# A hybrid RWKV and attention layer: strict order in the RWKV preparation, late output weights split on VectorE, a joint to the up phase without GpSimd

## The chip, the cores and the metric

The kernel runs on one core of one Trainium2 chip. A core has five engines that run side by side: TensorE (PE in the profile, with weight loads apart as PEld), VectorE (DVE), ScalarE (ACT), GpSimd (POOL) and SyncE (SP), which here only issues DMA transfers. The metric is device time in microseconds (us) of one execution. The kernel before took a median of 1824.77 us over three runs (1822.93 to 1825.58).

## The reference

One layer of a decoder trunk, for 1024 tokens of width 1024, in fp32:

```python
h = rms_norm(x, norm1_g)
proj = h @ w_in                       # RWKV, stick-breaking, memory query, gates
y_a = rwkv7_branch(p_rwkv, ...)       # token shift, decay, delta-rule state, 8 heads x 64
y_b = stick_breaking_branch(p_sb, ...)           # 8 heads x 64
y_m = memory_branch(q_mem, mem, ...)             # 256 memory tokens, 4 heads x 128
branch_out = einsum('btnc,ncd->btnd', stack(y_a, y_b, y_m), w_branch)
gates = sigmoid(gate_logits)
x = x + sum(gates * branch_out, axis=2) @ w_out
x = x + conv_ffn(x, ...)   # norm, w_up (5632), causal conv of width 3, silu(gate) * value, w_down
```

In the RWKV branch each token has a decay, a receptance r, a key k, a value v and a normalised key direction kk; the state is updated by `S = S*w + (S @ -kk) (kk*a) + v k`, and the output also gets a bonus, `sum(r*k*r_k) * v`, before a gate g.

## The kernel before

**Arithmetic.** Every large product is made of three products in the fast fp32r type: an operand is split into a high part, rounded by ACT (`Copy` into an fp32r tile), and a low part, the difference, made by DVE or POOL. `mm3` issues high x high, high x low and low x high. A 128 x 1024 weight tile is loaded by SP (`load_w`), rounded by ACT and differenced by POOL (`split_raw`, L82).

**Stages.** After a start of some 50 us, `rwkv_prep` runs four cycles, one for each pair of heads (p = 0 to 3), each a Python generator. `weave` runs it one step at a time, and after each step it takes one step of a filler stream, the projections of `x`: a filler step is mostly six matmuls, one eighth of a projection's contraction, and eight of them end a projection. So PE has six filler matmuls for each `yield` in `rwkv_prep`. From 310 us on attention, memory attention, gates and the RWKV state run in the same manner (the middle), then `branch_last` and `out_proj`, then the joint, where the up projection of the ConvFFN begins while the last tokens are still being normalised, and from about 1235 us a steady up phase and the down phase.

**One preparation cycle.** `k`, `a`, the decay and its running sum `cc` (a scan on DVE) give P and Q (exponentials on ACT). A column sum on PE, a power on POOL and `expand_heads` on DVE give the key's norm; `bcast_heads` broadcasts it over rows by eight transposes on PE (L113) into PSUM. Then DVE makes `kk` (L386) and `b` (L387). For each half h of the 1024 tokens `chain` makes two operands, `bk` (four multiplies of 64 x 512, L396) and `ra` (L397 to L399), and `gram` multiplies them, eight small matmuls for each quarter f, into PSUM, which DVE multiplies by a mask (L413) and three DMAs write out. `decayed` (POOL, L425) and `turned` (eight transposes) make a transposed operand. The bonus is two matmuls, two multiplies (L446) and a fused add (L447). `shifted` (L257) drains a projection: two multiplies out of PSUM (L263), an ACT scale, and the token shift's last operation on DVE (L266), here called the tail. All PSUM tiles that are not projections share one tag `g` of four banks.

**What sets the order.** A scheduler places the instructions of each engine by dependence and priority. `pinned` (L115) keeps a marked instruction in the program's order, and while `strict` is set it also chains it behind the last pinned one of its engine; before, `strict` was set only for the state stage. Most of PE's work is pinned. [...]

**Output weights.** `load_wo(k)` loads and splits the eight `w_out` tiles; the last four (k from 4) are loaded late and their lows run on POOL. `branch_last` ends with the merge: DVE multiplies the branch product by the gate (L1230), adds (L1235) and makes lows (L1242, tile `mg`).

**Up phase.** `w_up` is multiplied by a two-level Strassen-like scheme: for a pair n of weight tiles seven products, written (n,1) to (n,7), each 12 matmuls of 128 x 512. Their activations are the operands `11`, `21`, `22`, `T1` to `T4`, made by sums of quarters (L1310) and split by `high` (ACT) and `low` (L1325, DVE or POOL); their names in the profile are `B` or `BT`. Weight sums (`sums2`, `sums3`) and splits (`hl`, L1415) run on POOL. `step(n, i)` issues a product and what drains it; `conv` makes the convolution and the activation. The joint is the hand-written sequence at the end of `up_phase` that runs pairs 0 and 1.

## Time and profile before

| | |
|---|---|
| median of 3 runs | 1824.77 us |
| the profiled execution | 1822.09 us |
| its span | 1820.3 us |
| mean granted PE clock | 0.996 of full speed |
| instructions | 27424 |

A row of a timeline gives the start, the duration, engine, line, operation, output and inputs with their shapes, how often, and in brackets the idle time before it with what ended it. Equal neighbouring instructions are drawn together as one row (x2, x24), whose duration is the whole stretch. A matmul row's duration is modelled and overlaps the next, so the cost of one is read from the distance between starts. A row of the view of waits gives the waiting engine and line, what it waited for, the sum in us, how often, and the longest.

### The profile page before, as it was taken

The numbers are of one execution on the slowest core, as the hardware profiler recorded it, in microseconds if no ns is written. First come the engines' busy times: TensorE is split into PE (matmuls) and PEld (weight loads), VectorE is DVE, ScalarE is ACT, GpSimd is POOL, SyncE is SP. The second block draws the span as 40 slices with busy tenths as digits, with TensorE's granted clock in tenths as the row PEclk, the third lists the DMA queues.
The fourth block names the chain that finished last, engine by engine and source line by source line (L and its number), as shares of the span: only waits on it lengthen the run. The fifth ranks groups of instructions, "written<-read, shape, count | busy, mean of one in ns | idle before, by whom it ended". The sixth has DMA issues, their size and how long they took to land.

```text
span 1820.3 us, 27424 instructions
## 1 busy us (share of the span) xinstructions
PE 1784.4 (98%) x10468; PEld 1444.0 (79%) x10468; DVE 1191.1 (65%) x1659; ACT 882.7 (48%) x1665; POOL 770.1 (42%) x441
## 2 busy tenths in 40 slices
PE   8999999999999999999999999989999999999999
PEld 6777778878888888787777878868888888888887
DVE  5657773988977515232634792597776777786497
ACT  5443352555666645543556543464444444544343
POOL 2322343222221362221333341476777767645454
PEclk9999999999999999999999999999999999999999
DMA  4155466111112352457864562323332333386475
GB/s 182 59 174 185 146 191 221 50 42 50 58 41 79 103 162 65 154 190 243 283 230 182 204 213 105 127 61 113 110 110 87 101 114 110 122 298 240 145 236 203
DMA packets 120613, 263.39 MB, mean 145 GB/s; under 512 B 28313, under 2 KB 40857, under 8 KB 120354
## 3 DMA queue, kind: packets, MB, share of 16 engines
q1 hardware_dynamic: 82722, 194.76, 32.6%
q10 hardware_dynamic: 33984, 54.27, 8.1%
q0 software_dynamic: 3776, 12.62, 2.2%
q8 instruction: 82, 1.34, 0.3%
q14 instruction: 49, 0.40, 0.1%
HBM read 180.04 MB, written 81.53 MB: 144 GB/s over the span
## 4 chain that ended last, share of the span: by engine, by line
PE 77%; DVE 12%; issue 4%; ACT 3%; POOL 2%; DMA 2%; ACTq 0%; SPq 0%; DVEq 0%; POOLq 0%
PE mm L130 63%; PE g L130 11%; PE g L113 3%; POOL dw L1687 1%; DVE it L479 1%; DVE at L872 1%; DVE inst L481 1%; DVE qk L396 1%; DVE qk L398 1%; DVE BT L1328 1%; DVE w L774 0%; DVE qk L819 0%; DVE at L1235 0%; DMA w<-mrd 0%; DVE qk L606 0%
## 5 line engine op out<-in xcount | busy, mean ns | idle before, releaser
L85 POOL TENSOR_TENSOR wl<-wr,wh 128x1024 fp32r<-128x1024 f32 x77 | 195.7, 2542 | 443.5 <-ACT wh L83 437.0
L130 PE MATMUL mm<-xhi,wh 128*128 128x512 f32 x784 | 263.3, 416 | 8.3 <-ACT xhi L199 7.3
L130 PE MATMUL mm<-xlo,wh 128*128 128x512 f32 x784 | 245.5, 395 | 0.9 <-DVE xlo L200 0.9
L130 PE MATMUL mm<-xhi,wl 128*128 128x512 f32 x784 | 243.6, 392 | 0.0
L130 PEld LDWEIGHTS mm<-xlo,wh 128*128 128x128 f32 x784 | 148.2, 189 | 34.5 <-DVE xlo L200 1.6
L130 PEld LDWEIGHTS mm<-xhi,wl 128*128 128x128 f32 x784 | 147.9, 189 | 33.8 <-POOL wl L85 0.9
L130 PEld LDWEIGHTS mm<-xhi,wh 128*128 128x128 f32 x784 | 137.1, 190 | 38.3 <-issue 8.8
L83 ACT ACTIVATE wh<-wr 128x1024 fp32r<-128x1024 f32 x77 | 81.5, 1059 | 91.4 <-PE mm L130 51.3
L130 PE MATMUL mm<-dw,da 128*128 128x512 f32 x528 | 120.8, 390 | 0.0
L130 PE MATMUL mm<-BT,l 128*128 128x512 f32 x504 | 117.7, 389 | 0.0
L130 PEld LDWEIGHTS mm<-dw,da 128*128 128x128 f32 x528 | 98.9, 188 | 21.3 <-DVE da L1686 0.8
L1687 POOL TENSOR_TENSOR dw<-draw,dw 128x512 fp32r<-128x512 f32 x55 | 82.3, 1505 | 77.4 <-ACT dw L1685 75.9
L130 PE MATMUL mm<-BT,wh 128*128 128x512 f32 x352 | 109.2, 390 | 2.9 <-DVE BT L1328 2.9
L130 PEld LDWEIGHTS mm<-BT,l 128*128 128x128 f32 x504 | 94.6, 188 | 19.6
L130 PE MATMUL mm<-B,wh 128*128 128x512 f32 x352 | 108.6, 390 | 1.5 <-DVE p L1518 1.5
L872 DVE TENSOR_TENSOR_SCAN at<-at,at 128x128 f32<-128x128 f32 (+3 forms) x64 | 90.0, 1407 | 27.9 <-ACT at L866 27.7
L1686 DVE TENSOR_TENSOR da<-draw,da 128x512 fp32r<-128x512 f32 x77 | 70.6, 928 | 47.6 <-ACT da L1684 47.2
L1419 POOL TENSOR_TENSOR l<-it,l 128x1024 fp32r<-128x1024 f32 x21 | 51.6, 2457 | 95.5 <-ACT l L1418 95.5
L130 PE MATMUL g<-dw,da 128*128 128x512 f32 x396 | 90.5, 389 | 0.3 <-POOL dw L1687 0.3
L1684 ACT ACTIVATE da<-draw 128x512 fp32r<-128x512 f32 x77 | 48.3, 628 | 82.9 <-PE mm L130 32.0
L774 DVE TENSOR_TENSOR w<-w,rbc 128x1024 f32<-128x1024 f32 x24 | 50.5, 2105 | 58.0 <-ACT w L773 54.7
L186 POOL TENSOR_TENSOR hf<-rs,half 128x16 f32<-128x16 f32 (+1 forms) x18 | 48.9, 2718 | 91.1 <-DVE rs L183 86.4
(329 smaller groups left out, 4021.3 us busy)
## 6 DMA issues: line engine op xcount, KB each, us to landing
wr<-in_w_in_dram SPq DMA_DIRECT2D x50, 512.0 KB, 3.6
draw<-actd SPq DMA_DIRECT2D x77, 256.0 KB, 3.5
at<-scr SPq DMA_DIRECT2D x28, 512.0 KB, 5.4
draw<-in_w_down_dram SPq DMA_DIRECT2D x55, 256.0 KB, 4.7
rw<-in_w_up_dram SPq DMA_DIRECT2D x22, 512.0 KB, 3.5
actd<-gall ACTq DMA_DIRECT2D x44, 256.0 KB, 3.4
gsd<-w ACTq DMA_DIRECT2D x20, 512.0 KB, 2.8
wr<-in_w_up_dram SPq DMA_DIRECT2D x20, 512.0 KB, 3.7
```

The lines of the kernel that those rows point to most:

```text
L83: ins = self.nc.scalar.activation(hi, raw, AF.Copy)
L85: self.nc.gpsimd.tensor_tensor(lo, raw, hi.bitcast(F32), ALU.subtract)
L113: self.pinned(self.nc.tensor.transpose(out, in_, self.ident[:n, :n]))
L130: self.pinned(self.nc.tensor.matmul(*a, **k))
L186: nc.gpsimd.tensor_tensor(out, t[:, :n], self.half[:, :n], ALU.pow)
L396: nc.vector.tensor_tensor(bk4[q, :, first ^ h2], self.c8(x[q, hs]), self.c8(Q[q, hs]), ALU.mult)
L774: nc.vector.tensor_tensor(g, g, self.rbc, ALU.mult)
L872: self.pinned(nc.vector.tensor_tensor_scan(sn[:, :W][:, ::-1], sn[:, :W][:, ::-1], self.smask[:, 1024 - W :][:, ::-1], 1.0, ALU.mult, ALU. ...
L1419: keep(eng.tensor_tensor(lo, src, hi.bitcast(F32), ALU.subtract))
L1684: self.pinned(nc.scalar.activation(A[:, 0], a, AF.Copy))
L1686: self.pinned(nc.vector.tensor_tensor(A[:, 1], a, A[:, 0].bitcast(F32), ALU.subtract))
L1687: nc.gpsimd.tensor_tensor(Wt[:, 1], w, Wt[:, 0].bitcast(F32), ALU.subtract)
```

## The change

It has four parts. Instruction counts on PE are the same before and after, and after the joint the order on every engine is the same again.

**1. Preparation.** The four cycles run with `strict` set, and all their ACT and DVE operations, and those of `shifted`, are pinned, so that each follows the one before it in program order. The tail of `shifted` is put off: it is queued in `tails` and run in the middle of the next projection (`finish_tails`). `chain` makes `ra` first, spills it, then `bk`, with a `yield` after each; the two bonus matmuls come right after the broadcast and the rest of the bonus after `bk`; both grams of a half (16 small matmuls) are issued together; a cycle takes 28 steps instead of 27.

```diff
 
-    def split_raw(self, raw, hi, lo):
+    def split_raw(self, raw, hi, lo, dve=False):
         ins = self.nc.scalar.activation(hi, raw, AF.Copy)
         self.behind(ins, self.last_fin)
-        self.nc.gpsimd.tensor_tensor(lo, raw, hi.bitcast(F32), ALU.subtract)
+        if dve:
+            ins = self.nc.vector.tensor_tensor(lo, raw, hi.bitcast(F32), ALU.subtract)
+            self.behind(ins, self.last_fixed[ins.ins.engine])
+        else:
+            self.nc.gpsimd.tensor_tensor(lo, raw, hi.bitcast(F32), ALU.subtract)
         return hi, lo
...
-        nc.vector.scalar_tensor_tensor(out, pr, self.omm[:, ti : ti + 1], tmp, ALU.mult, ALU.add)
+        finish = lambda: self.pinned(nc.vector.scalar_tensor_tensor(out, pr, self.omm[:, ti : ti + 1], tmp, ALU.mult, ALU.add))
+        if self.pin:
+            self.tails.append(finish)
+        else:
+            finish()
...
+    def finish_tails(self):
+        while self.tails:
+            self.tails.pop(0)()
...
             if k == 3:
+                self.finish_tails()
                 self.settle()
...
+        bcs = self.bcast_heads(ex)
+        pbs = []
+        for hs in halves:
+            pbs.append(self.ps("g"))
+            self.mmul(pbs[-1], self.blk, rk[:, hs], start=True, stop=True)
...
+        def chain(h, out):
...
+            stt(ra4[:, :, 1, 1:64], self.c8(P[:, hs])[:, :, 0:63], -1.0, self.c8(kk[:, hs])[:, :, 1:64], ALU.mult, ALU.mult)
+            self.pinned(nc.vector.tensor_scalar(ra4[:, :, 1, 0], self.c8(kk[:, hs])[:, :, 0], -math.exp(OFF), None, ALU.mult))
+            tt(ra4[:, :, 0], self.c8(r[:, hs]), self.c8(P[:, hs]), ALU.mult)
+            self.spill(p, h, 0, ra, nc.sync)
+            yield
...
-            nc.vector.tensor_tensor(ra4[:, :, 0], self.c8(r[:, hs]), self.c8(P[:, hs]), ALU.mult)
-            nc.vector.scalar_tensor_tensor(ra4[:, :, 1, 1:64], self.c8(P[:, hs])[:, :, 0:63], -1.0, self.c8(kk[:, hs])[:, :, 1:64], ALU.mult, ALU.mult)
...
-            return bk, ra
...
-        def gram(h, f, bk, ra):
...
+        def gram(h, bk, ra):
+            pms = []
+            for f in range(2):
+                pm = [self.ps("g"), self.ps("g")]
+                for c in range(4):
+                    o = (f * 4 + c) * 128
+                    for h2 in range(2):
+                        q = slice(h2 * 64, h2 * 64 + 64)
+                        self.mmul(pm[h2][:, c * 128 : (c + 1) * 128], bk[q, o : o + 128], ra[q, o : o + 128], start=True, stop=True)
+                pms.append(pm)
...
-        u0 = chain(0)
+        u0, u1 = [], []
+        yield from chain(0, u0)
+        yield
         bp = decayed(0, u0[0])
...
+        for hs, pb in zip(halves, pbs):
+            tt(bon[:, hs], pb, v[:, hs], ALU.mult)
...
-        for _ in range(4):
-            yield
-        gram(0, 0, *u0)
-        yield
-        gram(0, 1, *u0)
-        u1 = chain(1)
+        yield
+        yield from gram(0, *u0)
+        rest = chain(1, u1)
+        next(rest)
+        yield
         turned(0, bp)
+        next(rest)
...
-        for _ in range(4):
-            yield
-        gram(1, 0, *u1)
-        yield
-        gram(1, 1, *u1)
+        yield
+        yield
+        yield from gram(1, *u1)
...
+        self.strict = True
         for p in range(4):
             self.weave(self.rwkv_prep(p, krv[p], need), pump, 1.0)
+        self.strict = False
```

On PE, the second cycle from the broadcast (`g<-kon,it`, transposes) to the gram (`g<-qk,qk`); `mm` rows are the filler's projections. Before:

```order
L113 MATMUL g_1115<-kon,it_1048 128x128 x4
L113 MATMUL g_1120<-kon,it_1048 128x128 x4
L130 MATMUL mm_1107<-xhi_114,wh_986 128x512
...
L130 MATMUL mm_1108<-xhi_125,wl_987 128x512
L130 MATMUL g_1152<-qk_1068,kon 128x512
L130 MATMUL g_1155<-qk_1068,kon 128x512
L130 MATMUL mm_1107<-xhi_138,wh_986 128x512
...
L130 MATMUL mm_1108<-xhi_171,wl_987 128x512
L130 MATMUL g_1187<-qk_1129,qk_1128 128x128
```

After:

```order
L117 MATMUL g_1120<-kon,it_1066 128x128 x4
L117 MATMUL g_1125<-kon,it_1066 128x128 x4
L134 MATMUL g_1130<-qk_1098,kon 128x512
L134 MATMUL g_1132<-qk_1098,kon 128x512
L134 MATMUL mm_1106<-xhi_125,wh_984 128x512
...
L134 MATMUL mm_1206<-xhi_102,wl_1103 128x512
L134 MATMUL g_1213<-qk_1144,qk_1143 128x128
```

Before, 36 filler matmuls and the two bonus matmuls (`g<-qk_1068,kon`) stand between broadcast and gram; after, 42, and the bonus matmuls (`g<-qk_1098,kon`) follow the broadcast directly.

On DVE, the same stretch, from `kk` (`at_720` or `at_718` with `params`) to the mask multiplies (`at<-g,kon`). Before:

```order
L386 SCALAR_TENSOR_TENSOR at_720<-at_720,params,g_1115 128x512
L386 SCALAR_TENSOR_TENSOR at_720<-at_720,params,g_1120 128x512
L387 TENSOR_TENSOR qk_965<-at_720,qk_965 128x1024
L396 TENSOR_TENSOR qk_1128<-qk_965,qk_966 64x8x64 x2
L446 TENSOR_TENSOR at_963<-g_1152,at_963 128x512
L266 SCALAR_TENSOR_TENSOR at_1099<-w_163_1093,omm,w_164_1094 128x1024
L446 TENSOR_TENSOR at_963<-g_1155,at_963 128x512
L397 TENSOR_TENSOR qk_1129<-at_852,qk_979 128x8x64
L398 SCALAR_TENSOR_TENSOR qk_1129<-qk_979,at_720 128x8x63
L447 SCALAR_TENSOR_TENSOR at_963<-at_963,params,qk_1038 128x1024
L399 TENSOR_SCALAR qk_1129<-at_720 128x8
L396 TENSOR_TENSOR qk_1232<-qk_965,qk_966 64x8x64 x2
```

After:

```order
L344 SCALAR_TENSOR_TENSOR at_718<-at_718,params,g_1120 128x512
L344 SCALAR_TENSOR_TENSOR at_718<-at_718,params,g_1125 128x512
L343 TENSOR_TENSOR qk_964<-at_718,qk_964 128x1024
L344 SCALAR_TENSOR_TENSOR qk_1144<-qk_978,at_718 128x8x63
L420 TENSOR_SCALAR qk_1144<-at_718 128x8
L343 TENSOR_TENSOR qk_1144<-at_832,qk_978 128x8x64
L270 SCALAR_TENSOR_TENSOR at_1080<-w_159_1074,omm,w_160_1075 128x1024
L343 TENSOR_TENSOR qk_1143<-qk_964,qk_965 64x8x64 x2
L343 TENSOR_TENSOR qk_1143<-qk_980,qk_965 64x8x64 x2
L343 TENSOR_TENSOR at_963<-g_1130,at_963 128x512
L343 TENSOR_TENSOR at_963<-g_1132,at_963 128x512
```

Before, a piece of `bk`, the bonus and a tail (L266) stand before the last piece of `ra` (L399). After, `ra` comes first, then one tail (L270) and the four pieces of `bk` (two rows x2), then the bonus (`at_963<-g`).

**2. Middle.** The four subtractions of `differ` (L698), which waited for their loads, become hooks on steps 3 to 6 of the first attention key projection; `spread_last` hangs on a step of a gate; the memory branch's column sums are split in two; a hook of `mem_q` moves from step 1 to 3.

```diff
-            nc.vector.tensor_tensor(v, v, raw, ALU.subtract)
...
+    def difference(self, i):
+        self.pinned(self.nc.vector.tensor_tensor(self.v[i], self.v[i], self.raw[i], ALU.subtract))
```

**3. Output weights.** The lows of the last four `w_out` tiles run on DVE, behind its last pinned operation, instead of on POOL (`split_raw`'s new argument, shown above).

```diff
-        self.wo.append(self.split_raw(self.load_w(self.I["w_out"][k], self.last_go if k > 3 else None), *hl))
+        self.wo.append(self.split_raw(self.load_w(self.I["w_out"][k], self.last_go if k > 3 else None), *hl, k > 3))
```

On DVE the four stand between the last `mg` lows and the first operation after `out_proj`'s first product (L1276); on POOL the four `L85` rows are gone.

**4. Joint.** For pairs 0 and 1 the weight sums and lows run on DVE instead of POOL; the copies `p1` of the first products move from DVE to ACT; the low of `T1` is made once in full width; those of `T3`, `22` and `T4` are interleaved with the weights' by halves; the loads of pair 2 are issued by ACT; `conv` for pairs 0 and 1 is pinned and its two halves are interleaved; product (2,1) moves ahead of (1,3); POOL's work on pair 2 starts after (1,6).

```diff
-                    nc.sync.dma_start(W[n][i], self.I["w_up"][m + i])
+                    if n == 2:
+                        self.pinned(nc.scalar.dma_start(W[n][i], self.I["w_up"][m + i]))
+                    else:
+                        nc.sync.dma_start(W[n][i], self.I["w_up"][m + i])
...
+        def engine(n):
+            return self.pinned if n < 3 else lambda ins: None, nc.vector if n < 2 else nc.gpsimd
...
         def sums2(n):
-            keep = self.pinned if n == 1 else lambda ins: None
+            keep, eng = engine(n)
             w1, w2 = W[n]
             s = st[n, "s"] = self.t4("it")
-            keep(nc.gpsimd.tensor_tensor(s[:, L], w2[:, L], w2[:, R], ALU.add))
...
                 p1 = st[n, "p1"] = self.r4("p1", n=512)
+                ins = nc.scalar.activation(p1, A, AF.Copy)
                 if n < 2:
-                    self.pinned(nc.vector.tensor_copy(p1, A))
-                else:
-                    nc.scalar.activation(p1, A, AF.Copy)
+                    self.pinned(ins)
...
+        step(1, 1)
         sums2(1)
+        late(7)
         hi("T1", old)
-        lo("T1", old)
-        step(1, 1)
-        sums3(1)
-        late(7)
-        hi("T3", old)
         sums(384, 512, (0,))
         hi("T2", new)
         lo("T2", new)
+        hi("T1", new)
+        lo("T1", full)
+        hi("T3", old)
         sums(384, 512, (1,))
-        hi("T1", new)
-        lo("T1", new)
...
-        for ts in (old, new):
-            lo("T3", ts)
+        lo1("T3", 0)
         prep3(0)
-        hi("22", slice(0, 512))
-        lo("22", slice(0, 512))
-        operand("T4", self.pool_a, "A", bufs=4)
+        lo1("T3", 1)
+        hi("22", full)
+        lo1("22", 0)
         step(0, 5)
         v = st[0, "u2"] = u_tile(True)
         self.pinned(nc.scalar.activation(v[:, R2], st[0, "C"], AF.Copy))
-        st[0, 3] = hl(self.early[3][:, R], self.pool_l, ("l4", "l4"), 512, True)
-        hi("T4", slice(0, 512))
-        lo("T4", slice(0, 512))
+        st[0, 3] = hl(self.early[3][:, R], self.pool_l, ("l4", "l4"), 512, True, nc.vector)
+        lo1("22", 1)
+        operand("T4", self.pool_a, "A", bufs=4)
+        hi("T4", full)
+        lo("T4", full)
+        prep2(1)
+        load(2)
         step(0, 7)
-        prep2(1)
+        sums3(1)
         u = step(0, 3)
-        prep3(1)
-        load(2)
...
-            order = (6, 5, 7, 4, 3) if n == 1 else (1, 5, 6, 2, 7, 4, 3)
+            order = {1: (6, 5, 7, 4, 3), 2: (5, 6, 2, 7, 4, 3)}.get(n, (1, 5, 6, 2, 7, 4, 3))
...
-                    step(n, i)
-                if n == 1 and i in (6, 5):
-                    conv(0, 1 if i == 6 else 0, v if i == 6 else u)
+                    u = step(n, i) or u
+                if n == 1 and i == 4:
+                    step(2, 1)
+                elif n == 2 and i == 6:
+                    conv(1, 0, u)
+                    act_sums(0, False)
+                elif n == 2 and i == 7:
+                    act_sums(0, True)
+                if n == 1 and i == 6:
+                    prep3(1)
+                    prep1(2)
+                    conv(0, 1, v)
+                elif n == 1 and i == 7:
+                    conv(0, 0, u)
+                    self.strict = False
```

On PE, the first matmul of each product from (1,7) on (each has twelve). Before:

```order
L130 MATMUL mm_10956<-BT_0_0_10724,wh_10930 128x512
...
L130 MATMUL mm_11040<-BT_0_0_10871,wh_10930 128x512
...
L130 MATMUL mm_10983<-B_0_0_10728,l_1748_10934 128x512
...
L130 MATMUL mm_11103<-B_0_0_10377,wh_11036 128x512
...
L130 MATMUL mm_11118<-BT_0_0_10720,l_1764_11016 128x512
```

After:

```order
L134 MATMUL mm_10944<-BT_0_0_10724,wh_10958 128x512
...
L134 MATMUL mm_11036<-BT_0_0_10884,wh_10958 128x512
...
L134 MATMUL mm_11060<-B_0_0_10377,wh_10966 128x512
...
L134 MATMUL mm_10983<-B_0_0_10728,l_1752_10962 128x512
...
L134 MATMUL mm_11099<-BT_0_0_10720,l_1763_11003 128x512
```

Before, (1,3) (`B_0_0_10728` with an `l` weight) is followed by (2,1) (`B_0_0_10377`); after, (2,1) stands first.

On DVE, the operands' lows. Before:

```order
L1328 TENSOR_TENSOR BT_1_0_10726<-A_10001,BT_0_0_10724 128x2x384
L1328 TENSOR_TENSOR BT_1_1_10727<-A_10002,BT_0_1_10725 128x2x384
L1328 TENSOR_TENSOR BT_1_0_10726<-A_10001,BT_0_0_10724 128x2x128
L1328 TENSOR_TENSOR BT_1_1_10727<-A_10002,BT_0_1_10725 128x2x128
L1419 TENSOR_TENSOR wl_10864<-wsec_10509,wh_10863 128x1024
L1328 TENSOR_TENSOR B_1_0_10730<-A_10003,B_0_0_10728 128x1024
L1328 TENSOR_TENSOR B_1_1_10731<-A_10004,B_0_1_10729 128x1024
L1328 TENSOR_TENSOR BT_1_0_10873<-raw_10000,BT_0_0_10871 128x1024
L1328 TENSOR_TENSOR BT_1_1_10874<-raw_10000,BT_0_1_10872 128x1024
L1542 TENSOR_TENSOR u_10888<-mm_10845,p_1728_10750 128x512
```

After:

```order
L1370 TENSOR_TENSOR BT_1_0_10726<-A_10001,BT_0_0_10724 128x1024
L1464 TENSOR_TENSOR wl_10856<-wsec_10509,wh_10855 128x1024
L1370 TENSOR_TENSOR BT_1_1_10727<-A_10002,BT_0_1_10725 128x1024
L1370 TENSOR_TENSOR B_1_0_10730<-A_10003,B_0_0_10728 128x1024
L1464 TENSOR_TENSOR l_1742_10880<-wsum_10510,l_1741_10879 128x512
L1370 TENSOR_TENSOR B_1_1_10731<-A_10004,B_0_1_10729 128x1024
L1370 TENSOR_TENSOR BT_1_0_10886<-raw_10000,BT_0_0_10884 128x1024
L1370 TENSOR_TENSOR BT_1_1_10887<-raw_10000,BT_0_1_10885 128x1024
L1464 TENSOR_TENSOR l_1744_10893<-it_10767,l_1743_10892 128x1024
L1592 TENSOR_TENSOR u_10876<-mm_10840,p_1728_10750 128x512
```

Before, three quarters and then quarters of `T3` (`BT_1_0_10726`) and one weight low (`wl`); after, full widths, with two weight lows more (`l<-wsum`, `l<-it`) that stood on POOL.

More of the change, by code (lines that the diff above doesn't have):

```diff
@@ L1583, in up_phase @@
         lo = lambda name, ts, eng=nc.vector: low(name, src[name], eng, ts)
-        self.pin = True
+        full = slice(0, 512)
+        lo1 = lambda name, j: low(name, src[name], nc.vector, full, (j,))
+        self.pin = self.strict = True
         load(1)
```

208 lines of the change are left out of this document (111 added, 97 removed).

## The prediction

> **What bounds the kernel now.** I read the page first, then the windows by stage, then what TensorE waited for in each stage, then the timelines of VectorE (DVE), GpSimd (POOL) and TensorE (PE) around those waits.
>
> ```profile
> PE 1784.4 (98%) x10468; PEld 1444.0 (79%) x10468; DVE 1191.1 (65%) x1659; ACT 882.7 (48%) x1665; POOL 770.1 (42%) x441
> ...
> 50.00:310.00 260.00, 250.78 (x1445) 193.50 (x1445) 164.75 (x202) 106.92 (x130) 82.94 (x38) 0.99 0.51 164
> 310.00:1060.00 750.00, 744.95 (x5521) 602.43 (x5521) 451.98 (x661) 406.16 (x963) 230.58 (x126) 1.00 0.41 136
> 1060.00:1235.00 175.00, 166.25 (x750) 135.57 (x749) 114.44 (x186) 77.28 (x146) 74.11 (x44) 0.99 0.34 116
> 1235.00:1820.30 585.30, 581.19 (x2560) 479.76 (x2558) 433.19 (x584) 265.06 (x396) 368.25 (x225) 1.00 0.46 153
> ```
>
> The last four rows are time, then busy time of PE, weight loads, DVE, ACT, POOL, then PE clock. PE is the bound. Both programs issue the same 7081 rows on PE, so only its idle time can change: 9.2 us in the preparation (260 less 250.78), 5.1 in the middle, 8.8 around output projection and joint, 4.1 in the rest. The first three, which the change touches, cap a gain at 23 us. The causes, as releaser: us in total, times, longest:
>
> ```profile
> PE g L113 <- DVE at L413: 6.4, 3, 2.6
> PE g L130 <- DVE qk L399: 2.4, 2, 1.8
> ...
> PE mm L130 <- DVE BT L1328: 2.9, 2, 1.7
> PE mm L130 <- DVE at L1230: 2.3, 1, 2.3
> PE mm L130 <- DVE p L1518: 1.5, 1, 1.5
> PE mm L130 <- DVE u L1547: 1.1, 1, 1.1
> PE mm L130 <- DVE wl L1419: 1.0, 1, 1.0
> ```
>
> All of it is DVE arriving late, in two places that the change rewrites. Why DVE is late there:
>
> ```profile
> 1076.60 4.95 DVE L1242 TENSOR_TENSOR mg<-at,mg 128x256 fp32r<-128x256 f32 x2 [0.55 <-ACT mg L1241]
> 1081.47 1.28 DVE L1235 TENSOR_TENSOR at<-at,w 128x512 f32<-128x512 f32 x2
> 1201.65 6.74 DVE L1328 TENSOR_TENSOR BT<-raw,BT 128x1024 fp32r<-128x1024 f32 x2
> 1197.13 1.22 DVE L1419 TENSOR_TENSOR wl<-wsec,wh 128x1024 fp32r<-128x1024 f32 x1
> 1177.92 0.42 DVE L1310 TENSOR_TENSOR A<-A,A 128x256 f32<-128x256 f32 x1
> ...
> 1076.34 2.40 POOL L85 TENSOR_TENSOR wo_sp<-wr,it 128x1024 fp32r<-128x1024 f32 x1 [9.56 <-ACT it L83]
> 1078.70 2.56 POOL L85 TENSOR_TENSOR qk<-wr,qk 128x1024 fp32r<-128x1024 f32 x1
> 1200.95 3.03 POOL L1419 TENSOR_TENSOR l<-it,l 128x1024 fp32r<-128x1024 f32 x1 [1.44 <-ACT l L1418]
> 1203.94 3.37 POOL L1419 TENSOR_TENSOR wl<-rw,wh 128x1024 fp32r<-128x1024 f32 x1
> ```
>
> Two quarter-width subtractions cost 4.95 us where others of that size cost 0.42 each; they end at 1081.55, just after POOL's two end (1081.26). Two full lows cost 6.74 instead of 2 x 1.22, ending a microsecond after POOL's second. [...]
>
> **Output projection.** Four output-weight lows leave POOL (2.40 and 2.56 above) and follow on DVE at 1.22 each, after the last merge low. Without POOL running, 4.95 becomes 0.84. The 4.1 us gained ahead of the product that waits on L1230 exceeds its 2.3. The new lows lie in DVE's idle time after its last merge work:
>
> ```profile
> 1104.53 1.29 DVE L1276 TENSOR_TENSOR w<-mm,w 128x512 f32<-128x512 f32 x2 [12.44 <-PE mm L130]
> ...
> 1089.60 5.60 PE L130 MATMUL mm<-at,mg 128*128 128x512 f32 x24
> 1095.04 0.62 PE L130 MATMUL mm<-it,mg 128*128 128x512 f32 x2
> ...
> wr<-in_w_in_dram SPq DMA_DIRECT2D x50, 512.0 KB, 3.6
> ```
>
> The merge work ended at 1104.53 - 12.44 = 1092.1; 4.1 shorter, at 1088. The first low follows by 1089.5, and PE wants that weight at 1095.04 - 2.3 = 1092.7. The third low needs the first one's raw buffer, a load (such loads land in 3.6 us) and ACT's rounding: near 1095.5, wanted 24 matmuls after the first, at 1098. Term: -2.2; bounds -2.3 and, if the load takes twice as long, +1. From 1089.60 to 1095.04 are 24 matmuls: 0.227 us each, used below.
>
> **Preparation.** Rows of the second of its four cycles:
>
> ```profile
> 138.47 1.03 PE L113 MATMUL g<-kon,it 128*128 128x128 f32 x8
> 142.08 1.88 PE L130 MATMUL g<-qk,kon 128*128 128x512 f32 x4
> 143.40 1.02 PE L130 MATMUL mm<-xhi,wh 128*128 128x512 f32 x2
> 151.16 1.16 PE L130 MATMUL g<-qk,qk 64*128 64x128 f32 x16 [1.75 <-DVE qk L399]
> ...
> 133.45 1.28 DVE L266 SCALAR_TENSOR_TENSOR at<-w,omm,w 128x1024 f32<-128x1024 f32 x1
> 139.10 1.41 DVE L386 SCALAR_TENSOR_TENSOR at<-at,params,g 128x512 f32<-128x512 f32 x2 [0.74 <-PE g L113]
> 140.54 1.22 DVE L387 TENSOR_TENSOR qk<-at,qk 128x1024 f32<-128x1024 f32 x1
> 141.80 1.39 DVE L396 TENSOR_TENSOR qk<-qk,qk 64x512 f32<-64x512 f32 x2
> 143.83 2.51 DVE L266 SCALAR_TENSOR_TENSOR at<-w,omm,w 128x1024 f32<-128x1024 f32 x1
> 146.86 2.28 DVE L397 TENSOR_TENSOR qk<-at,qk 128x512 f32<-128x512 f32 x1
> 149.66 1.27 DVE L447 SCALAR_TENSOR_TENSOR at<-at,params,qk 128x1024 f32<-128x1024 f32 x1
> ```
>
> DVE is busy from 139.10 to 151.0, with bonus work (1.27 and two halves of 0.7) and two blocked operations (2.51, 2.28) ahead of the gram's last operand, while PE has 36 matmuls (8.2 us) plus the bonus products (1.3): hence 1.75. In the new order the bonus follows both operands. What stands before the gram: 1.41 + 1.22, the three pieces of ra (some 0.7 + 0.2 + 0.7, from the 512-wide row), one tail 1.28, four bk pieces 2.78: 8.3 us. PE covers it by 42 x 0.227 = 9.5 plus 1.3: about 2.5 us to spare. The other stall, transposes waiting on the mask multiplies (L413), has 18 matmuls (4.1 us) where it had 12 (2.7), and multiplies with nothing movable between them. POOL still runs here, so one collision (up to 2.4) can eat that spare now and then: I leave 1.5 of the 9.2. Term: -7.7; bounds -9.2 and 0.
>
> **Joint.** The early pairs' sums and lows move from POOL to DVE: at 512 columns 0.64 (half of 1.28) four times, two lows of 1.22, two of about 0.62, 6.2 us together; two copies of p1 (0.7 each) go to ACT. DVE saves 4.3 on 6.74 and 3.1 on
>
> ```profile
> 1183.75 3.94 DVE L1328 TENSOR_TENSOR BT<-raw,BT 128x768 fp32r<-128x768 f32 x2 [0.77 <-ACT BT L1323]
> 1198.27 3.45 DVE L1328 TENSOR_TENSOR B<-A,B 128x1024 fp32r<-128x1024 f32 x2
> ```
>
> (3.94 less twice three quarters of 1.22, 3.45 less 2 x 1.22). So DVE works 6.2 - 1.4 - 7.4 = 2.6 us less, and the lows that the products want first come first, by halves. That removes the 2.9 on BT and, with the copy on ACT, the 1.5. The wait on u (1.1) is covered by 12 matmuls of the next pair (2.7 us) put ahead of the product that waits. The 1.0 on wl stays, with some 0.5 where POOL begins pair 2. Term: 6.5 - 1.5 = -5.0; bounds -6.5 and 0.
>
> **Middle.** The hooks move little. DVE's queue loses the waits in which a subtraction stood at its head:
>
> ```profile
> DVE A L698 <- DMA A<-vsd: 23.3, 3, 9.9
> ...
> 300.00:500.00 200.00, 197.02 (x1335) 160.63 (x1334) 180.85 (x168) 110.56 (x195) 55.40 (x24) 0.99 0.17 54
> ```
>
> Right after, DVE is 90% busy (180.85 of 200) with the inverse, so its order matters there, but PE idled only 3.0 us. Term 0; bounds -3 and +5 (rival two).
>
> **Sum.** -2.2 - 7.7 - 5.0 = -14.9. The profiled execution took 1822.1 us (span 1820.3), so 1807.2; the median of the runs, 1824.8, is 2.7 above it: **1810**. With each term between a third less and its full bound, 1804 to 1816.
>
> **Rivals.**
> One: collisions refill the preparation. Eight gram halves each meet POOL operations of about 2.4 us with 2.5 to spare; if half do beyond it, 4 x 2.3 = 9.2 returns, giving 1810 + 7.7 = 1818. Against: POOL is busy 82.94 of 260 us.
>
> Two: the stalls move rather than go. DVE bounds 300 to 500: each cycle now takes 28 steps of filler instead of 27, so four steps of six matmuls (5.4 us) of cover leave the DVE-bound stretch, and the four subtractions (1.2 each, 4.9) enter it. All unabsorbed: 10.3 us, 1820 to 1821; with a joint that gains nothing, 1825, no change. Against: DVE has 19 us idle there, and gets 23.3 earlier.
>
> Three, slower: the strict order makes DVE and ACT wait at the head of their queues. A drain that waits for a product's end now stands ahead of the broadcast, decay or gram that PE wants next, which formerly could pass. There are 12 such places (a broadcast and two grams in each of four cycles). If each costs what the transposes wait on average now (6.4 / 3 = 2.1), that is 25.6 instead of 9.2: +16.4 - 7.2 = +9.2, so 1834. It decides from 1.4 us a place: 12 x 1.4 is what preparation loses now (9.2) and what the rest gains (7.2). Against: the drains' products end 12 matmuls or more before. [...]
>
> **Chances.** Forecast 0.62, one 0.12, two 0.10, three 0.16. What a measurement can tell from no change is 0.2%, 3.6 us: 1821 to 1828. Faster: forecast, one, and a third of two: 0.77; same: most of two and a little of three, 0.08; slower 0.15. The range that leaves out 2 in 10 reaches from 1803 over rivals one and two to 1826.
>
> **What would show it.** Right: the waits of PE from 50 to 310 sum to about 1.5, none on the mask multiplies beyond 1 us; 4.95 and 6.74 gone from DVE's rows; the product after 1081 starting without a wait; the second pair's last products some 15 us earlier; span near 1805. Wrong: waits on broadcast or gram in several cycles (three), transposes still waiting 2 us with POOL beside (one), PE waiting on inverse or normalisation rows between 300 and 500 (two), or a first wait of the steady up phase, which has none now, because POOL's weights for pair 2 come late.

## The result, and the profile after

The changed kernel takes **1801.88 us** (median of 4 runs, 1801.07 to 1803.86); the kernel before, on the same chip, took 1825.17 us (4 runs, 1822.93 to 1828.65). The ratio is **0.9872** (0.9854 to 0.9890). It is faster, as forecast, but by 23 us where 14.8 were forecast, a microsecond beyond the range. The profiled execution took 1802.59 us, its span 1800.8 us: 19.5 us less than the span before. Ratios compare fast runs alone: two runs far outside, one of 3576 us in a1 and one of 1998 us of the kernel before beside a0 and a4, are left out.

The page's busy line and the windows of the same stages (time, busy PE, weight loads, DVE, ACT, POOL, then PE clock) for the changed kernel:

```profile
PE 1777.1 (99%) x10468; PEld 1442.6 (80%) x10468; DVE 1177.0 (65%) x1665; ACT 882.6 (49%) x1667; POOL 743.8 (41%) x429
...
50.00:310.00 260.00, 258.05 (x1508) 203.40 (x1507) 163.80 (x212) 111.51 (x134) 89.51 (x40) 1.00 0.54 169
310.00:1060.00 750.00, 743.70 (x5517) 601.44 (x5516) 454.57 (x669) 405.55 (x966) 230.45 (x125) 1.00 0.41 138
1060.00:1235.00 175.00, 172.68 (x783) 141.92 (x783) 114.87 (x196) 84.08 (x154) 57.95 (x38) 0.99 0.34 115
1235.00:1800.80 565.80, 561.65 (x2472) 463.12 (x2470) 417.83 (x563) 254.42 (x382) 351.78 (x217) 1.00 0.46 154
```

PE's idle time in the preparation fell from 9.2 to 2.0 us, and around output projection and joint from 8.8 to 2.3. But PE's busy time fell too, from 1784.4 to 1777.1, with the same 10468 instructions. That is the part that the prediction has no term for. A stage's gain can be read by looking up the same instruction of PE in both traces; this table is called the ledger below:

```
same instruction on PE, start in us     before     after    gained in the stage
early in the first cycle                 58.07     58.80    -0.7
past the preparation                    327.11    313.73    14.1
ahead of output projection             1031.53   1019.18    -1.0
in output projection, all weights there 1108.63  1091.79     4.5
past the joint                         1284.50   1264.65     3.0
end of the span                        1820.3    1800.8     -0.4
```

What PE waits for in the preparation, and in output projection and joint together (us in total, times, longest), in the changed kernel:

```profile
PE mm L134 <- POOL wl L89: 1.3, 1, 1.3
PE g L117 <- DVE w L284: 0.7, 1, 0.7
...
PE mm L134 <- DVE u L1598: 2.0, 1, 2.0
```

The waits on mask multiplies, gram operands, L1230 and `BT` are all gone. Three are new: 1.3 us of a filler product on a weight low of POOL (at 255.26), 0.7 on L284, behind the last cycle, and 2.0 on `u`. The collisions of DVE with POOL went as read; the two full lows of 6.74 us, and the merge lows of 4.95, in DVE's timeline after:

```profile
1182.74 2.35 DVE L1370 TENSOR_TENSOR BT<-raw,BT 128x1024 fp32r<-128x1024 f32 x2
...
1065.12 0.76 DVE L1284 TENSOR_TENSOR mg<-at,mg 128x256 fp32r<-128x256 f32 x2 [1.39 <-ACT mg L1283]
```

**Where busy time went: the clock.** PE's windows in the kernel before (time, busy PE, clock), around three places:

```profile
149.40:152.81 3.41, 1.66 (x19) 1.00 0.81 273
152.82:156.22 3.40, 3.40 (x19) 0.50 0.90 337
...
309.83:313.23 3.40, 3.40 (x10) 0.50 0.22 93
1081.24:1084.64 3.40, 1.14 (x4) 1.00 0.69 202
1084.66:1088.06 3.40, 3.40 (x10) 0.50 0.00 0
```

Three times TensorE was granted half of its clock for 3.41 us, though it was busy throughout: 3.41 x 0.5 = 1.7 us lost each time. Such a time is called a slow stretch below. The first stands behind the 1.75 us wait on the gram (first row), the last behind the 2.26 us wait on L1230 (fourth row). The one at 309.83 stands behind no wait, but behind 64 matmuls of 2 or 4 columns in a row. PE's timeline before, then after:

```profile
307.36 1.10 PE L130 MATMUL g<-kon,ys 8*64 8x4 f32 x32
308.38 1.10 PE L130 MATMUL g<-kon,w 128*64 128x2 f32 x32
```

```profile
289.80 1.10 PE L134 MATMUL g<-kon,ys 8*64 8x4 f32 x32
295.15 1.10 PE L134 MATMUL g<-kon,w 128*64 128x2 f32 x32
```

After the change the two bursts are 5 us apart, and no slow stretch follows. So the preparation's 14.1 us are 6.7 of idle time (9.2 to 2.5 between the two instructions of the ledger), 3.4 of clock at 152 and 309, 3.1 of switching (experiment a2), and 0.9 that I can't place. Each trace has one more slow stretch in the middle (617.02 before, 683.88 after), and the changed kernel one in the joint. Which stretches a run gets is partly chance: between 50 and 330 us e2 and e3, with the old preparation, have three and two, not all at these places, and in e3 the two bursts in a row are followed by full clock. But the changed kernel and its seven repeats and variants have none there.

**The new wait.** Product (2,3) in the changed kernel; PE, then DVE, then POOL:

```profile
1218.99 4.58 PE L134 MATMUL mm<-B,l 128*128 128x512 f32 x12 [2.03 <-DVE u L1598]
```

```profile
1213.68 3.83 DVE L1551 TENSOR_TENSOR gall<-gall 128x512 f32<-128x512 f32 x2
...
1218.15 0.69 DVE L1598 TENSOR_TENSOR u<-mm,u 128x512 f32<-128x512 f32 x1
```

```profile
1191.27 2.62 POOL L1464 TENSOR_TENSOR wl<-wr,wh 128x1024 fp32r<-128x1024 f32 x1 [26.01 <-ACT wh L1463]
...
1212.88 2.39 POOL L1464 TENSOR_TENSOR l<-it,l 128x1024 fp32r<-128x1024 f32 x1
1215.34 1.62 POOL L1480 TENSOR_TENSOR it<-wr 128x512 f32<-128x512 f32 x1
```

Two activation sums (L1551, `act_sums(0, False)`) stand ahead of the drain of (2,7) and take 3.83 us beside POOL's operations, where the shortest of that line took 0.68; PE waits for the drain, and its next 12 matmuls take 4.58 instead of 12 x 0.227 = 2.7. POOL, idle for 26 us in the joint, now does pair 2 there. So the joint gives back 3.7 us (2.0 and 1.7) of what its old waits gave, and the ledger's 3.0 is what is left.

### The profile page after: what moved, and what is told of

Its sections match the earlier page's. It is cut to its first block, busy times and chain, and to the rows that moved or that the text cites. A ratio compares the mean times of both kernels' runs of the same rounds, so it can differ in the third digit from the quotient of the medians.

```text
span 1800.8 us, 27440 instructions
## 1 busy us (share of the span) xinstructions
PE 1777.1 (99%) x10468; PEld 1442.6 (80%) x10468; DVE 1177.0 (65%) x1665; ACT 882.6 (49%) x1667; POOL 743.8 (41%) x429
## 4 chain that ended last, share of the span: by engine, by line
PE 86%; DVE 6%; issue 3%; POOL 2%; DMA 2%; ACT 1%; SPq 0%; POOLq 0%; DVEq 0%; ACTq 0%
PE mm L134 71%; PE g L134 12%; PE g L117 4%; POOL dw L1753 1%; DVE at L903 1%; DVE it L506 1%; DVE inst L508 1%; DMA mrd<-w 0%; DMA w<-mrd 0%; DVE qk L849 0%; POOL w L1217 0%; DVE qk L848 0%; DVE gall L1540 0%; DMA at<-in_xT_dram 0%; DMA w<-gsd 0%
## 5 line engine op out<-in xcount | busy, mean ns | idle before, releaser
L134 PEld LDWEIGHTS g<-dw,da 128*128 128x128 f32 x396 | 74.2, 188 | 16.2 <-POOL dw L1753 0.8
```

The source lines that it names most:

```text
L134: self.pinned(self.nc.tensor.matmul(*a, **k))
```

## The experiments

The e kernels are the kernel before with parts of the change, the a kernels the changed one with an edit; a3 and a6 add work that the output doesn't use. The edits of e1, e4, e2 and e3 together are the whole change. Gains in us are worked out from the ratio, with 1824.7 as the time before.

**e1_prep**: preparation alone, with `differ` (the four subtractions of the middle) as it was.

```diff
...
+        self.strict = True
         for p in range(4):
             self.weave(self.rwkv_prep(p, krv[p], need), pump, 1.0)
+        self.strict = False
```

> The kernel before with the preparation part of the change alone (strict order, tails, chain and gram reordered); output weights, middle hooks and joint as before. Theory of the slow clock: a long wait of PE costs more than itself, because the granted clock stays low after it, and the gram issued in one group instead of two saves switches of PE between product kinds; then this part alone is worth 13 to 15 us (time about 1811 where before is 1825), and the windows of the preparation show no stretch with a clock of 0.6 to 0.7. Theory of the prediction: only the listed waits go, -7.7 us (about 1817). Theory of combination: the four subtractions still stand at the head of DVE's queue and wait for their loads, so less than 5 us is gained.

1816.87 us, ratio 0.9953 (0.9941 to 0.9966): -8.6 us. By the ledger it was 10.2 ahead at 214 us and only 8.0 at 327. PE's waits from 50 to 330, and what DVE did before the longest:

```profile
PE g L130 <- DVE qk L339: 2.7, 3, 2.2
PE g L113 <- DVE w L280: 1.6, 1, 1.6
PE g L130 <- ACT w L849: 1.2, 1, 1.2
```

```profile
249.90 2.92 DVE L722 TENSOR_TENSOR A<-A,w 128x1024 f32<-128x1024 f32 x1 [5.04 <-DMA A<-vsd]
252.75 1.21 DVE L339 TENSOR_TENSOR qk<-at,qk 128x1024 f32<-128x1024 f32 x1
```

A subtraction waited 5.04 us for its load at the head of DVE's queue, took 2.92, and the last cycle's gram operands queued behind it. A slow stretch followed the 2.2 us wait on the gram (at 258.92). The 1.2 us wait stands right ahead of a burst of 32 tiny matmuls, and another slow stretch followed these (at 320.36). The changed kernel is 10.5 ahead at 214 and 13.4 at 327: without the hooks, the last part of that is lost. No run separates the strict order from the new order of `chain`, bonus and tails.

**e4_mid**: the middle's hooks alone.

```diff
-            nc.vector.tensor_tensor(v, v, raw, ALU.subtract)
...
+    def difference(self, i):
+        self.pinned(self.nc.vector.tensor_tensor(self.v[i], self.v[i], self.raw[i], ALU.subtract))
...
+        kh = {} if p else {k: functools.partial(self.difference, k - 3) for k in (3, 4, 5, 6)}
...
```

> The kernel before with the middle's hooks alone (the four subtractions as hooks, spread_last on a gate, memory column sums split, one mem_q hook later). Slow clock and prediction alike: within 1.5 us of before, PE's waits from 310 to 1060 us stay at 4 to 7 us in sum. Combination: the hooks are what frees DVE ahead of the inverse, -3 us or more.

1823.13 us, 0.9986 (0.9977 to 0.9995): -2.6, where my term was 0. The hooks also part the two bursts (301.34 and 306.69 in its trace), and no slow stretch follows there. The mean granted clock of its 11 runs is 0.9977, that of the 19 runs before beside them 0.9961: about 3 us, the size of the gain. (Its one trace is no shorter than that before, as the wait on L1230 took 4.0 us there and the slow stretch at it 6.83.)

**e5_prep_mid**: both together.

> The kernel before with preparation and middle of the change, without the output weights' and the joint's part. Alone the two measured 0.9953 and 0.9986 of before, together 0.994 if they only add (about 1813.5). Theory of combination, after the profile of the preparation alone: a subtraction at the head of DVE's queue waits for its load ahead of the fourth cycle's kk, and PE waits 2.3 us on the gram and 3 us on the attention norm behind it; with the hooks those waits go, so this kernel is at 0.991 to 0.993 (1808 to 1812), its PE is 13 to 15 us ahead of before at 320 us, and no wait on qk L339 or w L280 is over 1 us. Theory of the prediction: 0.9958 (about 1817).

1809.54 us, 0.9910 (0.9893 to 0.9927): -16.4. The two ratios multiplied give 0.9939, so together they are worth about 5 us more than apart. The intervals overlap a little (the product's reaches down to 0.9918), so it is the trace that decides: e5 is 13.3 us ahead at 327, as the changed kernel is, and DVE has no wait on the subtractions' loads there (e1: 14.9 us in 3 waits). The middle's hooks belong to the preparation's gain.

**e2_wout**: the output-weight lows alone.

```diff
...
-        self.wo.append(self.split_raw(self.load_w(self.I["w_out"][k], self.last_go if k > 3 else None), *hl))
+        self.wo.append(self.split_raw(self.load_w(self.I["w_out"][k], self.last_go if k > 3 else None), *hl, k > 3))
```

> The kernel before with the lows of the last four output weights on VectorE, and nothing else of the change. Slow clock: the wait of 2.3 us goes and with it the 6 us after it at a clock of 0.72, together -4.5 us. Prediction: -2.2 us. Combination: near 0, because the stall moves to a later product.

1820.49 us, 0.9972 (0.9960 to 0.9983): -5.1 us, not -2.2. PE has no wait left between 1010 and 1115, and the ledger gives 4.4 over that stretch. A 2.26 us wait and the 1.7 us lost in the slow stretch behind it make 4.0. The wait is also larger in most runs: 3.8, 3.9, 4.0 and 3.4 in the traces of e1, e3, e4 and e5, which have this code as before. The profiled execution before, with 2.26, was a mild one.

**e3_joint**: the joint alone.

```diff
+        def engine(n):
+            return self.pinned if n < 3 else lambda ins: None, nc.vector if n < 2 else nc.gpsimd
...
+            keep(eng.tensor_tensor(s[:, L], w2[:, L], w2[:, R], ALU.add))
+            keep(eng.tensor_tensor(s[:, R], s[:, L], w1[:, L], ALU.subtract))
...
```

> The kernel before with the joint's part of the change alone. Slow clock: -3 to -3.5 us, made of about -7 from the waits that go and +3.9 from one new wait at product (2,3) (2.2 us, and 1.7 us of slow clock behind it), seen in the waits as PE on DVE u L1551 or so at the last product of pair 2. Prediction: -5.0 us without that new wait. Combination: 0 or slower, since the POOL work on the output weights is still there.

1821.48 us, 0.9981 (0.9970 to 0.9991): -3.5. Its waits from 1030 to 1260:

```profile
PE mm L130 <- DVE at L1230: 3.9, 1, 3.9
PE mm L130 <- DVE u L1556: 2.0, 1, 2.0
```

The new 2.0 us wait is there without the rest of the change: it belongs to the joint. The parts multiply to 0.9910 x 0.9972 x 0.9981 = 0.9863, the whole is 0.9872 and, on another chip (**a0_after**, the changed kernel again), 0.9886 (0.9870 to 0.9901).

> The changed kernel itself, on the same chip beside a4: 0.987 of before (about 1802), with its wait of 2.0 us at product (2,3) and nine slow matmuls behind it.

It took 1802.42 us there, beside a4, which shares its chip.

**a3_ladder**: made waits in the steady up phase, to measure what a wait does to the clock. ACT copies a tile 2 to 18 times, and one tiny matmul waits for it:

```diff
+                steps = {4: 2, 5: 4, 6: 6, 7: 9, 8: 13, 9: 18, 11: 2, 12: 4, 13: 6, 14: 9, 15: 13, 16: 18}.get(n, 0)
+                if steps:
+                    sc = self.small("sc", [128, 64], bufs=1)
+                    for _ in range(steps):
+                        nc.scalar.activation(sc, A[:, 0:64], AF.Copy)
+                    self.mmul(self.ps("g")[0:64, 0:1], sc, self.ones[:, 0:1], start=True, stop=True)
```

> The changed kernel with twelve made waits in the steady up phase: after product 1 of pairs 4 to 9 and 11 to 16, PE waits for 2, 4, 6, 9, 13 and 18 small copies on ACT (128 x 64) through one added tiny matmul whose result is not used; the output is the same. Theory of the slow clock: behind waits up to about 1.5 us PE goes on at full clock, behind those over some 2 us a stretch of 3.5 to 4.5 us follows at 0.6 to 0.7 of the clock, which costs 1.7 to 2.1 us whatever the length of the wait. Rival one: the loss grows with the wait (half of it, say). Rival two: no low clock at all here, the low stretches belong to the preparation's and output projection's DMA load.

One run, 1864.95 us. Four of the waits in PE's timeline, and the windows right behind each:

```profile
1247.30 0.28 PE L134 MATMUL g<-kon,sc 128*64 128x1 f32 x2 [2.02 <-ACT sc L1572]
1270.09 0.28 PE L134 MATMUL g<-kon,sc 128*64 128x1 f32 x2 [1.64 <-ACT sc L1572]
...
1342.89 0.38 PE L134 MATMUL g<-kon,sc 128*64 128x1 f32 x2 [5.00 <-ACT sc L1572]
...
1433.92 0.28 PE L134 MATMUL g<-kon,sc 128*64 128x1 f32 x2 [2.53 <-ACT sc L1572]
```

```profile
1247.50:1252.10 4.60, 4.60 (x16) 0.65 0.17 63
1270.30:1275.00 4.70, 4.70 (x23) 1.00 0.04 16
...
1343.20:1347.80 4.60, 4.60 (x12) 0.50 0.01 3
...
1434.10:1438.70 4.60, 4.60 (x22) 1.00 0.18 70
```

A 0.65 here is a mean: in narrower windows the clock is 0.50 from 1248.92 to 1252.32, and 1.00 around it. Over all twelve: behind 0.57 and 1.64 us it stays at 1.00; behind 2.02, 2.15, 2.91, 3.04 and 3.81 it is 0.50 for 3.41 us, so 1.7 us are lost; at 3.93, 5.00, 5.91 and 6.28 it is 0.50 for 6.83 us, which begin within the wait, and 2.3 to 3.0 us are lost behind it; but behind 2.53 once it stays at 1.00. The DMA share (column after the clock) is 0.00 or 0.01 in six of the nine slow windows, so it isn't transfers.

**a6_tiny**: is it the wait or low activity? Bursts of tiny matmuls in place of the waits.

```diff
...
+                tiny = {4: 8, 5: 16, 6: 24, 7: 32, 8: 48, 9: 64, 11: 32, 12: 16, 13: 48, 14: 24, 15: 32, 16: 64}.get(n, 0)
+                pt = self.ps("g") if tiny else None
+                for _ in range(tiny):
+                    self.mmul(pt[0:64, 0:2], self.sc, self.ones[:, 0:2], start=True, stop=True)
```

> The changed kernel with bursts of small matmuls (64 stationary columns, 2 moving columns, of no use to the output) behind the first product of pairs 4 to 9 and 11 to 16: 16, 32, 48, 64, 96, 128 and 64, 32, 96, 48, 64, 128 instructions, some 0.034 us each by the row of 32 that took 1.10, so bursts of 0.55 to 4.4 us in which TensorE is never idle in the record. Theory: the clock falls by low activity, not by a wait as such, which is why the two adjacent bursts of 32 at 307.36 to 309.41 in the kernel before were followed by 4.5 us at 0.62, and the hooks of the middle, which put fillers between them, saved 1.7 us. Then the bursts of 64 and more (2.2 us and up) are followed by a clock near 0.63 and those of 128 near 0.50 for some 4.5 us, those of 16 and 32 by 1.00, as behind the waits of the ladder. Rival: only a wait lowers the clock, and the slow stretch at 309.41 had another cause; then the matmuls behind every burst keep 1.00.

One run, 1883.99 us. PE's timeline, the first four bursts, and the windows behind them:

```profile
1245.89 1.09 PE L134 MATMUL g<-kon,sc 128*64 128x2 f32 x16
...
1266.17 2.03 PE L134 MATMUL g<-kon,sc 128*64 128x2 f32 x32
...
1289.02 2.96 PE L134 MATMUL g<-kon,sc 128*64 128x2 f32 x48
...
1312.77 4.23 PE L134 MATMUL g<-kon,sc 128*64 128x2 f32 x64
```

```profile
1246.90:1251.50 4.60, 4.60 (x22) 1.00 0.53 198
1268.20:1272.70 4.50, 4.50 (x14) 0.62 0.06 24
1291.90:1296.40 4.50, 4.50 (x15) 0.62 0.28 102
1316.90:1321.40 4.50, 4.50 (x12) 0.50 0.00 0
```

An instruction took 0.065 us where I had put 0.034, so bursts came out twice as long as expected; by their length they do what waits of that length do, with PE never idle. The other bursts of 2.96 us and more (up to 11.16) were all followed by half clock too; a second burst of 2.03 us (at 1442.32) by full clock. The rival, that only a wait lowers the clock, falls.

**a2_gram_split**: the grams issued in two groups again, with six fillers between.

```diff
                 pms.append(pm)
+                if f == 0:
+                    yield
...
-                yield
+                if f == 1:
+                    yield
```

> The changed kernel with each gram issued as two groups of 8 small matmuls, six filler matmuls between them, as before; the same number of steps. Theory of the switches: going from a filler matmul to the gram costs 0.32 us and back 0.20 where filler to filler is 0.23 and gram to gram 0.06, so 8 more groups cost 8 x (0.32 + 0.20 - 0.23 - 0.06) = 1.9 us in the preparation with no new wait. Rival (the gain of grouping is that masks come earlier): new waits of transposes on the mask multiplies, 1 to 2 us each. Prediction: 0.

1804.38 us, 0.9886 (0.9872 to 0.9900); a1, on the same chip, has 1802.62. The medians alone don't settle it, the trace does: no wait was added from 50 to 330 us, and by the ledger the kernel falls 3.1 us behind the changed one over the preparation, little by little; for eight halves that is 0.39 us each. The rows of one half, in the changed kernel and in a2:

```profile
148.89 2.06 PE L134 MATMUL g<-qk,qk 64*128 64x128 f32 x32
```

```profile
149.61 1.16 PE L134 MATMUL g<-qk,qk 64*128 64x128 f32 x16
```

32 small matmuls in one go take 2.06, two groups of 16 take 2 x 1.16, and each group also costs a gap where PE turns from and to the fillers (in the changed kernel 0.32 us from the last filler's start to the gram's, where fillers start 0.23 apart). The spans differ by only 1.5. By the ledger 0.9 came back little by little between 314 and 1200 us. In the joint the 2.03 us wait was not followed by a slow stretch, which gave 1.5 back, but two waits of 0.3 and 0.9 at the next products took 1.3 of it again.

**a1_sums_late**: the two sums behind the drain that PE waits for.

```diff
                     conv(1, 0, u)
-                    act_sums(0, False)
                 elif n == 2 and i == 7:
+                    act_sums(0, False)
                     act_sums(0, True)
```

> The changed kernel with one thing moved: the first half of pair 0's activation sums (two operations of 0.69 us on DVE that took 3.83 beside POOL) stands behind the drain of product (2,7) instead of ahead of it. Theory of the slow clock: PE's wait of 2.2 us at product (2,3) goes and the 1.7 us of low clock behind it too, -3 to -4 us against the changed kernel (about 1798). Theory that a wait costs only itself: -2.2 (about 1799.7). Rival: the sums collide with the next POOL operation and the wait only moves to pair 3: within 1 us of the changed kernel (1801.9).

1802.62 us, 0.9876 (0.9859 to 0.9893): no gain. The wait on `u` is gone, and another stands four microseconds later, in PE's waits; then DVE's four sums:

```profile
PE mm L134 <- POOL wl L1464: 2.7, 1, 2.7
```

```profile
1215.79 7.71 DVE L1551 TENSOR_TENSOR gall<-gall 128x512 f32<-128x512 f32 x4
```

From 1223 to 1228 the mean clock was 0.66. Now POOL is late beside the sums (its two lows take 5.58 us where two take 4.76 at 1239.97, and the two additions ahead of them 1.62 and 1.73 instead of 1.30), and PE waits for POOL. **a4_pool_early** adds an earlier start of POOL on pair 2; **a5_pool_only** has that start alone:

```diff
-            if n > 1:
+            if n > 2:
                 sums2(n)
...
                     prep3(1)
+                    sums2(2)
                     prep1(2)
-                    conv(0, 1, v)
+                    conv(0, 1, v, lambda: prep2(2))
...
-                if i == (6 if n > 1 else 5):
+                if n > 1 and i == 6:
                     prep2(nxt)
```

> The changed kernel with the sums moved as in a1 and, as well, POOL's work on pair 2 taken forward: its weight sums (2 operations) ahead of its first low, and the rounding of the sums on ACT between the two halves of pair 0's convolution instead of behind it. In a1 the wait of 2.7 us at pair 3 came because POOL worked without a gap from 1191 us on and ended 2.7 us late. Theory that POOL's late start is the bound of the joint: POOL ends its weights for pair 3 four to five us earlier, no wait of PE over 1 us is left between 1180 and 1300, nor the low clock behind it, and the time is 3 to 4.5 us under a0_after (about 1798). Rival: POOL's sums now collide with DVE's last joint lows, PE waits 1 to 2 us at product (1,7) instead, with low clock or without: within 1.5 us of a0_after.

> The changed kernel with POOL's earlier start of a4, and the activation sums where the change has them. In a4 PE's wait moved to pair 4, behind DVE, whose four sums in one piece took 7.4 us beside POOL's two lows. Here the first two sums meet POOL's short additions (1.3 us each) instead of a low (2.4), so DVE drains product (2,7) some 1.5 to 2 us earlier than in the change. Theory that the wait at (2,3) is this one collision: it falls from 2.0 to under 0.7 us, the clock stays up, the time is 2.5 to 4 us under the changed kernel's 1802.4. Rival (DVE's and POOL's work in the joint is the bound, whatever its order): a wait of 1 to 2 us stands somewhere between 1215 and 1260 us again, within 1.5 us of the changed kernel.

a4: 1802.44 us, 0.9885 (0.9867 to 0.9902); a5: 1802.42 us, 0.9886 (0.9870 to 0.9903). Neither differs from the changed kernel. a4 has a wait of 2.2 us on the same drain as a5 (L1523), with a slow stretch behind it. a5's waits in the joint, and the sums beside POOL:

```profile
PE mm L134 <- DVE u L1523: 2.2, 1, 2.2
PE mm L134 <- DVE u L1600: 0.4, 1, 0.4
```

```profile
1212.69 2.97 DVE L1553 TENSOR_TENSOR gall<-gall 128x512 f32<-128x512 f32 x2
...
1216.91 5.62 DVE L1553 TENSOR_TENSOR gall<-gall 128x512 f32<-128x512 f32 x2
```

```profile
1216.78 5.20 POOL L1464 TENSOR_TENSOR wl<-rw,wh 128x1024 fp32r<-128x1024 f32 x2
```

The wait fell from 2.0 to 0.4, and 2.2 us came back a pair later (L1523, at 1233 us), here without a slow stretch. In three orders the same work on DVE and POOL, side by side, is late by some 2 us or more at one product or another. So these orders moved the wait and did not remove it; that no order does better isn't shown.

## Why the prediction was right in direction and short in size

**Right.** DVE arriving late was the cause, and the collisions were read rightly: 4.95 and 6.74 became 0.76 and 2.35. The waits of PE from 50 to 310 came out at 2.0 (forecast about 1.5), none on the mask multiplies; output projection lost its wait; the joint lost those on `BT` and the copy.

**Short.** Of the 8.1 us between 1810 and 1801.9, 4.6 are in the sum (-14.9 against -19.5 by the spans). By its terms:

```
                     predicted   measured (ledger)
preparation            -7.7        -14.1
middle                  0           +1.0
output projection      -2.2         -4.5
joint                  -5.0         -3.0
start and end           0           +1.1
```

The step that failed is the one at the head of the working: "both programs issue the same 7081 rows on PE, so only its idle time can change", from which idle times that "cap a gain at 23 us" follow. PE's busy time fell by 7.3 us with the same 10468 rows in the traces: the same instructions also run at half clock behind a stall, and cost more when split into more groups (0.39 us for each in a2). Two slow stretches fewer (3.4) and the switching (3.1) make 6.5 of the 7.3. The other runs agree: the mean granted clock is 0.9961 over the 19 runs before beside e1 to e4 and 0.9984 over eight of the changed kernel, which is 4.2 us. The preparation's term was sized as idle time alone, and its bound of -9.2 was no bound. Idle time itself came out near, 6.7 us against 7.7; what the term left out are 3.4 us of clock and 3.1 of switching. Output projection left out 1.7 of clock behind its wait: "exceeds its 2.3" was right about the cover and short about the price. The term for the middle was near, but e4 and e5 show that its hooks earn their part inside the preparation.

The joint's term was too large: it took the wait on `u` to be covered by 12 matmuls put ahead of (1,3). There it was, but the drain of the next pair, behind two sums and beside a POOL at work again, brought 2.0 us and 1.7 of clock that the term lacks. The prediction named POOL's late weights for pair 2 as what might come; in the changed kernel it was DVE's drain, and POOL's weights came late only when a1 moved the sums.

The other 3.5 us are the step from profile to median: I added 2.7, as the run before lay below its median, but the changed kernel's median lies 0.7 below its profiled run. e1, e3, e4 and e5 show a reason on one side: the wait on L1230 was 3.4 to 4.0 us in their traces, 2.26 in the profile that I summed against. That this explains all of the 3.5 isn't shown. In the range of the sum, a third less of each term gives 1814.9 rather than 1816, which changes nothing here.

**Rivals.** One: PE's waits did not refill, but for the 1.3 us on a weight low of POOL. Two: the middle lost 1.0 us of the 10.3, and at the sign that was named: PE's waits on normalisation rows (`hn`) between 300 and 500 grew from 1.08 and 1.13 us to 1.47 and 1.78. Three: of the 12 places of the strict order none waits; the 0.7 us on L284 stands at 303.95, behind the last cycle. Without the hooks, e1 shows what a head-of-queue wait does there: 2.2 us at one gram.

## What to carry to other kernels

Price a stall of TensorE of about 2 us or more with the slow stretch that may follow it, 1.7 us here: a bound made of idle time alone is too tight, and a stall of 2 us removed can be worth nearly twice its length (4.4 us by the ledger of e2 for a wait of 2.26). Tiny matmuls, of 2 or 4 moving columns, counted as a stall when they came in a row for 2 us (2.05 us at 307.36 in the kernel before, 2.03 at 1266.17 in a6), so put full ones between them. The small matmuls of a gram (64 x 128 by 64 x 128) did not: eight groups of about 2.06 us in the changed kernel kept full clock, and splitting them cost 0.39 us for each further group. Where two engines share the work ahead of TensorE, moving one operation of it can just hand the wait on: a1, a4 and a5 changed where, not how much.

## What the runs showed of the hardware that I had not expected

- In the fourteen traces the granted clock is 1.00 or 0.50. Ahead of a kernel's end a slow stretch lasts 3.41 us, or two to four times that, and within one trace all of them begin whole multiples of 3.41 us apart (152.81, 309.82, 617.02 and 1084.65 in the kernel before: 46, 90 and 137 times 3.4133).
- In these traces half clock goes with how much of the 3.41 us step ahead of it PE loses. From 12 us on, the last steps apart, each of the 35 steps at full clock with 2.0 us or more of waits and of matmuls of at most 4 columns was followed by half clock, none of the 7249 steps with less than 1.57, and 13 of the 35 in between. It fits that waits and bursts around 2 us went either way: the 1.75 us wait at 151.16 in the kernel before lies within one step, with small matmuls behind it, and the 2.57 us wait at 269.93 is parted between two (1.50 and 1.06 us). This is a count over the traces; no run moved a wait along the steps. The steps around 269.93 (time, busy PE, clock):

```profile
265.45:268.86 3.41, 1.91 (x9) 1.00 0.78 287
268.86:272.27 3.41, 2.35 (x14) 1.00 0.85 262
272.28:275.68 3.40, 3.40 (x17) 1.00 1.00 353
```

- Tiny matmuls (64 stationary, 2 moving columns) act on the clock as idle time does, while the record shows PE fully busy: in a6 the clock was 0.62 over 4.5 us behind one burst of 2.03 us, 1.00 behind another, and 0.50 behind 4.23 us, as behind waits of 2.02 us (0.65) and 5.00 us (0.50) in a3.
- Breaking a group of small matmuls in two cost 0.39 us with no wait in the record.
